# Attention probabilities of a scan-and-attention stage turned by 16-bit transposing transfers instead of TensorE

## The chip, the cores and the metric

One core of a Trainium2 chip runs the whole program. The metric is device microseconds (us) of one execution. The kernel before was timed in three runs: 1071.51, 1073.46 and 1073.56 us, median 1073.46 us. The profile is of one more execution, with a time of its own.

## The reference, cut to what matters

The program is one residual block of a streaming encoder on 512 tokens of width 1024: a feed-forward half step, two token mixers side by side, an output projection, a second feed-forward half step, a norm. The change lies in the mixers, which share one input projection `p = h @ w_in`.

```python
# mixer A: RWKV-7, 8 heads x 64, state carried forward in time
state = state * w_t + (state a_t) b_t + v_t k_t ;  y_t = state r_t
# mixer B: forgetting attention, 8 heads x 64, blocks of 128 queries
s = einsum('bhqd,bhkd->bhqk', q_i, k) * scale
s = s + c_i[..., :, None] - cum[..., None, :]       # cumulative log-forget bias
pr = softmax(where(mask, s, -inf))
out = einsum('bhqk,bhkd->bhqd', pr, v)
x = x + (sigmoid(g_A) * (y_A @ P_A) + sigmoid(g_B) * (y_B @ P_B)) @ W_out
```

All is float32. A product wanted at that accuracy is made as three products of high and low halves (`whi`, `wlo` of a weight; `xh`, `xl` of the activations).

## The kernel before, in words

The change touches one stage, in which three things run together on one core:

- the scan of mixer A, 16 chunks of 32 tokens in a chain: `product_x`, `copy_x`, `product_u`, `copy_u`, `products_sy`, `scale_s`. TensorE and, in turn, VectorE or ScalarE hand each other one small tile (`spot`, `Xs`, `RD`).
- the attention of mixer B: four pairs of heads `p`, each with blocks of queries taken together as `(0, 1)`, `(2,)` and `(3,)`; inside a block the two heads are `q` = 0 and 1. That makes 12 blocks of two heads. A block has `w` = 384, 384 or 512 columns of keys. For one head the steps are `logits` (TensorE, into a PSUM tile `l`), `maximum` (VectorE, `mx`), `exp` (ScalarE, into `pts`), `divide` (VectorE, in place on `pts`), a transposition so that keys lie on the partitions, and `values` (TensorE, with `tr` and the values `vt`). `pts` has one buffer per head `q`, so the `exp` of a head's next block waits until the probabilities of the block before have left it. I call the way from one `exp` to the next `exp` of the same head a round; each head place `q` has 12.
- fills: 13 columns of `w_in` (`pq` for queries and keys, `pgt` for gates), 24 matmuls of 128x512 each. A column's weights come by an SP transfer into `raw`, ScalarE casts the high half (`whi`), VectorE subtracts (`wlo`).

Before the change the transposition is done on TensorE (`turn`: one transpose of 128x128 against `ident` for every 128 columns, into the PSUM tile that held the logits), and ScalarE copies the result to SBUF (`copy_t`). That is the ordinary form: 80 transposes and 24 copies.

Order: the stage is written as a list of operations (`plan.op`), and the table `ORDER` says in which order they are put into the program. TensorE, VectorE and ScalarE run exactly in that order; the costs handed to `op` are used only by whoever searched the table. The queues of GpSimd (POOL) and SyncE (SP) run in order too: SP carries the weight loads, the second half of `Tall` (`fetch`, eight small transfers after chunks 3 and 7), and prefetches for the next stage; POOL carries the stores of gates (`gsave<-gs`) and prefetches (`G<-gsave`, `ga<-gsave`) into tiles that the scan gives up. A waiting instruction holds back all that stand behind it in its queue. `PLACES` names the PSUM bank that each `spot` and `l` gets. Since most operations go through one helper, their line in the profile is L103; the names of the tiles tell them apart.

Transposing transfers are not new to the kernel. The feed-forward stages (L804) and the token-wise copy of the residual (`tokens`, L1099 to L1107) use them: a float32 tile is taken apart into two planes of 16-bit halves, one transfer on SP turns both, and the halves are joined again.

Of the kernel before, what the change touches and what calls it, by code (L numbers as in the profile page):

```python
# [9 lines left out]
F32 = mybir.dt.float32  # L10
F32R = mybir.dt.float32r
BF16 = mybir.dt.bfloat16
U16 = mybir.dt.uint16
# [6 lines left out]
P = 128  # L20
T = 512
D = 1024
KD = D // P
# [4 lines left out]
C = 32  # L28
# [20 lines left out]


ORDER = [int(n) for n in """
# [23 lines left out]
""".split()]  # L75
PLACES = {
    "pr": "0211021000210120210202202102010110120102020202202121010201001002012202100020210",
    "pf": "0120120022102102001201210201",
}


# [1 line left out]
def kernel(  # L83
# [6 lines left out]
    nc = tc.nc  # L90
# [64 lines left out]
    loads = []  # L155

    def load_raw(aps, kt, n):
        raw = wp.tile([P, kt, n], F32, tag="raw", name="raw", bufs=3)
        for c0, src in aps:
            loads.append(nc.sync.dma_start(raw[:, :, c0:c0 + src.shape[1]],  # L160
                                           src.rearrange("(k p) c -> p k c", p=P)))
        return raw
# [37 lines left out]
    def f32(ap):  # L200
        return ap.bitcast(F32)
# [4 lines left out]
    def on(do, *a):  # L206
        return lambda: do(*a)
# [884 lines left out]
    def win(c0, n=P):  # L1092
        return [(0, W[:, c0:c0 + n])]
# [15 lines left out]
    with ExitStack() as mx:  # L1109
# [447 lines left out]
                pool.tensor_copy(Ds[i][half(q), :, q, :],  # L1557
                                 ident[half(q), half(q)].unsqueeze(1).broadcast_to([64, NP, 64]))

        plan = Plan(pr=3, pf=2, pm=1, w=1, raw=3, t=4, gs=2, tr=2, Xs=2)  # L1560
        op = plan.op
        summed, gone = [op("SP", 0.0, None, later=us, frees=frees) for us, frees in ((3.0, ()), (3.5, ["w"]))]
        o = op("ACT", 0.69, b1.log, summed, rank=SCAN, takes=["t"], frees=["pf"])
# [131 lines left out]


        ready, weighed = {0: [summed], 1: [rooted]}, []

        class Held:
            pass  # L1700

        def weights(at):
            w = Held()

            def load():
                w.raw = load_raw(win(at), KD, P)

            def high():
                w.hi, w.lo = [wp.tile([P, KD, P], F32R, tag=tag, name=tag, bufs=2) for tag in ("whi", "wlo")]
                act.copy(w.hi[:], w.raw[:])  # L1710

            def low():
                dve.tensor_tensor(w.lo[:], w.raw[:], f32(w.hi[:]), op=ALU.subtract)

            o = op("SP", 0.05, load, rank=FILL, takes=["raw"], later=4.0 if len(weighed) > 2 else 0.0)
            o = op("ACT", 0.99, high, o, *weighed[-1:], rank=NEXT, takes=["w"])
            weighed.append(op("DVE", 1.18, low, o, rank=NEXT, frees=["raw"]))
            return w, weighed[-1]
# [71 lines left out]

        pts = t2.tile([P, 2, T], F32, tag="pt", name="pts")
        qb = [rp.tile([P, T], F32R, name="qb0", tag="la"), t2.tile([P, T], F32R, name="qb1", tag="qb1")]
        sees, turned, exps, copies, yb = [], ([], []), [], [], []

        class Pair:
# [38 lines left out]
        class Block:  # L1834

            def __init__(s, pair, bl):
                s.pair, s.bl = pair, bl
                s.at = {b: sum(c + 1 for c in bl[:j]) * P for j, b in enumerate(bl)}
                s.w = sum(b + 1 for b in bl) * P
                s.lp, s.tr = [None] * 2, [None] * 2  # L1840

            def logits(s, q):
                s.lp[q] = whole("pf", pf)
# [22 lines left out]
            def divide(s, q):  # L1866
                sums = s.pair.mx[q][:, NB + s.bl[0]:NB + s.bl[-1] + 1]
                dve.reciprocal(sums, sums)
                for b in s.bl:
                    n, _, sum_ = s.of(q, b)  # L1870
                    dve.tensor_scalar(pts[:, q, n], pts[:, q, n], sum_, None, op0=ALU.mult)

            def turn(s, q):
                for k in range(s.w // P):
                    pe.transpose(s.lp[q][:, k * P:(k + 1) * P], pts[:, q, k * P:(k + 1) * P], ident[:])

            def copy_t(s, q):
                s.tr[q] = t2.tile([P, T], F32, tag="tr", name="tr", bufs=2)
                act.copy(s.tr[q][:, 0:s.w], s.lp[q][:, 0:s.w])

            def values(s):
                for j, b in enumerate(s.bl):
                    for k in range(b + 1):
                        o = s.at[b] + k * P
                        for m in range(0, P, C):
                            h = s.pair.p * P + m
                            pe.matmul(s.lp[1][m:m + C, j * P:(j + 1) * P], vt[k][:, h:h + C],
                                      s.tr[m // 64][:, o:o + P], start=k == 0, stop=k == b, tile_position=(0, m))

            def copy_o(s):  # L1890
                dve.tensor_copy(s.pair.qp[:, s.bl[0] * P:(s.bl[-1] + 1) * P], s.lp[1][:, 0:len(s.bl) * P])

            def enter(s, operands):
                for q in range(2):
                    us = sum(0.455 * (b + 1) * P / T + 0.06 for b in s.bl)
                    sees.append(op("PE", us, on(s.logits, q), *operands[q], rank=SIDE, takes=["pf"]))
                lit = sees[-2:]
                for q in range(2):
                    o = []
                    for b in s.bl:  # L1900
                        n = (b + 1) * P
                        e = op("DVE", 0.15 + 1.07e-3 * n, on(s.maximum, q, b), lit[q], rank=SIDE)
                        o.append(op("ACT", 0.265 + 0.85e-3 * n, on(s.exp, q, b), e, *turned[q][-1:], rank=SIDE))
                    exps.extend(o)
                    us = 0.19 + sum(0.14 + 0.525e-3 * (b + 1) * P for b in s.bl)
                    o = op("DVE", us, on(s.divide, q), *o, rank=SIDE)
                    lit[q] = op("PE", 0.11 * s.w / P, on(s.turn, q), o, rank=SIDE, kind="t")
                for q in range(2):
                    turned[q].append(lit[q])
                o = [op("ACT", 0.08 + 0.82e-3 * s.w, on(s.copy_t, q), lit[q], *copies[-1:], rank=SIDE, takes=["tr"],  # L1910
                        frees=["pf"] * (1 - q)) for q in range(2)]
                copies.append(o[1])
                us = 0.248 * sum(b + 1 for b in s.bl)
                o = op("PE", us, s.values, *o, rank=SIDE, frees=["tr"] * 2, kind="m")
                return op("DVE", 0.08 + 1.06e-3 * len(s.bl) * P, s.copy_o, o, rank=SIDE, frees=["pf"])

        outs = []
# [306 lines left out]
```

## Time and profile before

| | |
|---|---|
| median of three runs | 1073.46 us |
| the profiled execution's own time | 1072.17 us |
| its span | 1070.5 us (1.7 us lie around it) |
| granted TensorE clock | 0.998 of full |
| the stage with the change | about 510 to 647 us |
| TensorE transposes of `pts` | 80, from 522.5 to 637.3 us |
| copies `tr<-l` on ScalarE | 24, 12.3 us busy |

How to read the profile: a row of the timeline gives start, length, engine, line, operation, tiles, count, and in brackets how long the engine was idle before and what released it. "PEld" is the load of a matmul's stationary operand, which overlaps the matmuls. A row of the chain gives start, length and what the chain of work that ended last was in. A row of stretches gives the busy time of each engine, then the granted clock, the share of the transfer engines and GB/s. "SPq" and "POOLq" are the queues' own work, the issuing of transfers.

### The profile page before, as it was taken

What the parts mean: (1) busy time and instruction counts of PE and PEld (TensorE: products, weight loads), DVE (VectorE), ACT (ScalarE), POOL (GpSimd) and SP (SyncE); (2) the same over time, 40 slices, a digit from 0 to 9 for tenths busy, and PEclk for the clock granted to TensorE, in tenths of its full rate; (3) what the DMA queues carried; (4) which work ended last, traced back from release to release, by engine and by line L of the source; (5) the groups of instructions that cost most, each with busy time, mean ns of one, the idle gap of its engine ahead of it and who ended that gap; (6) DMA issues with size and microseconds to landing.
All of it is one profiled execution on the core that took longest, in us unless ns stands there. A gap on an engine that the chain in (4) does not pass through costs nothing.

```text
span 1070.5 us, 16775 instructions
## 1 busy us (share of the span) xinstructions
PE 1060.1 (99%) x6234; PEld 868.1 (81%) x6234; DVE 830.6 (78%) x1155; ACT 719.1 (67%) x1123; POOL 224.2 (21%) x275
## 2 busy tenths in 40 slices
PE   9999999999999999999999999999999999999997
PEld 7888888888887887888888787888888888888886
DVE  7997776789865698878777777866798766799874
ACT  6768767775655766445888876554578768676554
POOL 1221220134203202312000121136311212114210
PEclk9999999999999999999999999999999999999999
DMA  7999999989946443444312344666979999979972
GB/s 213 262 190 230 225 205 250 201 195 186 235 119 174 111 114 101 131 128 119 89 47 73 100 129 147 190 170 160 296 186 210 205 235 225 207 211 201 236 188 80
DMA packets 180112, 186.57 MB, mean 174 GB/s; under 512 B 50110, under 2 KB 116222, under 8 KB 180030
## 3 DMA queue, kind: packets, MB, share of 16 engines
q1 hardware_dynamic: 145902, 113.92, 37.0%
q0 software_dynamic: 33392, 70.14, 34.2%
q10 hardware_dynamic: 736, 1.45, 0.4%
q8 instruction: 49, 0.80, 0.3%
q14 instruction: 33, 0.27, 0.1%
HBM read 163.51 MB, written 12.52 MB: 164 GB/s over the span
## 4 chain that ended last, share of the span: by engine, by line
PE 86%; DVE 7%; ACT 3%; issue 2%; DMA 2%; SPq 0%; DVEq 0%; POOL 0%; ACTq 0%; POOLq 0%
PE P L103 32%; PE P L175 6%; PE P L177 6%; PE P L176 6%; PE pgt L103 5%; PE l L103 3%; PE spot L103 3%; PE pq L103 3%; PE ppj L103 2%; PE pk L175 2%; PE pk L177 2%; PE pk L176 2%; PE pw L176 1%; PE pw L175 1%; PE pw L177 1%
## 5 line engine op out<-in xcount | busy, mean ns | idle before, releaser
L103 PE MATMUL P<-sraw,q 128*128 128x512 f32 x344 | 91.3, 389 | 0.0
L103 PEld LDWEIGHTS P<-sraw,q 128*128 128x128 f32 x344 | 64.6, 188 | 13.4
L103 PE MATMUL P<-swhi,q 128*128 128x512 f32 x224 | 71.4, 390 | 0.1
L167 ACT CAST whi<-raw 128x1024 fp32r<-128x1024 f32 (+2 forms) x42 | 40.4, 961 | 45.2 <-issue 14.2
L103 PE MATMUL P<-sraw,wxh 128*128 128x512 f32 x200 | 67.7, 390 | 0.0
L103 PE MATMUL P<-swhi,wxh 128*128 128x512 f32 x144 | 56.6, 393 | 0.0
L168 DVE TENSOR_TENSOR wlo<-raw,whi 128x1024 fp32r<-128x1024 f32 (+2 forms) x43 | 48.5, 1127 | 10.4 <-ACT whi L167 9.1
L103 PE MATMUL P<-swhi,wxl 128*128 128x512 f32 x144 | 56.1, 390 | 0.0
L103 PE MATMUL P<-swlo,wxh 128*128 128x512 f32 x144 | 56.1, 389 | 0.0
L693 POOL DMA_DIRECT2D cb<-in_ffn_w_dram x20 | 24.1, 1207 | 145.8 <-DVE cd L103 78.4
L103 PE MATMUL P<-sraw,wxl 128*128 128x512 f32 x136 | 52.9, 389 | 0.0
L693 POOL DMA_DIRECT2D cd<-in_ffn_w_dram x24 | 29.3, 1221 | 112.6 <-DVE sraw L103 59.0
L103 PEld LDWEIGHTS P<-swhi,q 128*128 128x128 f32 x224 | 42.0, 188 | 9.2 <-DVE q L103 0.6
L103 DVE TENSOR_TENSOR u<-P,u 128x512 f32<-128x512 f32 x52 | 33.3, 682 | 13.7 <-ACT u L103 13.7
L103 PEld LDWEIGHTS P<-sraw,wxh 128*128 128x128 f32 x200 | 37.5, 188 | 7.7
L103 PE MATMUL P<-swlo,q 128*128 128x512 f32 x112 | 43.6, 389 | 0.0
L103 ACT COPY RD<-spot 32x128 f32<-32x128 f32 (+2 forms) x128 | 39.9, 312 | 5.3 <-PE spot L103 2.3
L552 POOL DMA_DIRECT2D ca<-in_ffn_w_dram x16 | 19.3, 1205 | 95.0 <-DVE swlo L103 65.6
L177 PE MATMUL pk<-xh,wlo 128*128 128x512 f32 x96 | 37.5, 392 | 1.0 <-DVE wlo L168 1.0
L175 PE MATMUL pk<-xh,whi 128*128 128x512 f32 x96 | 38.1, 396 | 0.4 <-DVE u L1257 0.4
L176 PE MATMUL pk<-xl,whi 128*128 128x512 f32 x96 | 37.4, 390 | 0.0
L177 PE MATMUL P<-swhi,wxl 128*128 128x512 f32 x96 | 37.3, 389 | 0.0
(630 smaller groups left out, 3435.2 us busy)
## 6 DMA issues: line engine op xcount, KB each, us to landing
raw<-in_w_in_dram SPq DMA_DIRECT2D x40, 512.0 KB
cc<-in_ffn_w_dram SPq DMA_DIRECT2D x36, 512.0 KB
cb<-in_ffn_w_dram POOLq DMA_DIRECT2D x36, 512.0 KB, 6.6
cb<-in_ffn_w_dram SPq DMA_DIRECT2D x32, 512.0 KB
cd<-in_ffn_w_dram POOLq DMA_DIRECT2D x32, 512.0 KB, 7.8
ca<-in_ffn_w_dram POOLq DMA_DIRECT2D x32, 512.0 KB, 8.4
ca<-in_ffn_w_dram SPq DMA_DIRECT2D x20, 512.0 KB
cd<-in_ffn_w_dram SPq DMA_DIRECT2D x18, 512.0 KB
```

What stands on the lines that cost most here:

```text
L103: q.last = do(*a, **kw)
L167: (hi_eng or act).copy(hi[:], raw[:])
L168: (eng or dve).tensor_tensor(lo[:], raw[:], hi[:].bitcast(F32), op=ALU.subtract)
L175: pe.matmul(ps, whi, xhi, start=first, stop=False, skip_group_check=onto)
L176: pe.matmul(ps, whi, xlo, start=False, stop=False, skip_group_check=onto)
L177: return pe.matmul(ps, wlo, xhi, start=False, stop=last, skip_group_check=onto)
L552: nc.gpsimd.dma_start(s.sum[g], src, accum_op=ALU.add)
L693: nc.gpsimd.dma_start(to, s.block(b, n, h), accum_op=ALU.add)
```

## The change

The transposition leaves TensorE. For each of the 24 block-and-head units:

1. `apart`, POOL: the float32 words of `pts` are copied as 16-bit halves into two planes (768 or 1024 halves per partition).
2. `turn`, SP: one transposing transfer writes the planes, turned, over `pts`.
3. `joined`: the halves are put together into `tr`, by VectorE for `q` = 0 and by ScalarE for `q` = 1.

The next `exp` of that head now waits for `joined`. The planes take one of the three `raw` buffers, so the weight columns keep two. `values` writes a PSUM tile of its own, so the tile of the logits is free after `exp`. `ORDER` and `PLACES` are replaced as a whole.

```diff
 ORDER = [int(n) for n in """
-172 1 191 173 0 174 6 175 379 176 374 11 192 372 373 177 178 7 179 381 375 376 14 5 210 377 378 380 12 8 9
...
+0 172 191 14 1 173 372 174 11 374 6 175 376 373 176 378 375 377 177 381 379 7 380 12 386 178 383 382 384 15
...
-        plan = Plan(pr=3, pf=2, pm=1, w=1, raw=3, t=4, gs=2, tr=2, Xs=2)
+        plan = Plan(pr=3, pf=2, pm=1, w=1, raw=2, t=4, gs=2, tr=2, Xs=2)
...
+        raws = [wp.tile([P, KD, P], F32, tag="raw", name="raw", bufs=3) for _ in range(3)]
+        planes = raws.pop().rearrange("p k t -> p (k t)").bitcast(U16).rearrange("p (q c) -> p q c", q=2)
...
+        JOIN, valued = ("DVE", "ACT"), []
...
+            def apart(s, q):
+                s.parts[q] = planes[:, q, 0:2 * s.w]
+                pool.tensor_copy(s.parts[q].rearrange("p (s c) -> p s c", s=2),
+                                 pts[:, q, 0:s.w].bitcast(U16).rearrange("p (c s) -> p s c", s=2))
+
             def turn(s, q):
-                for k in range(s.w // P):
-                    pe.transpose(s.lp[q][:, k * P:(k + 1) * P], pts[:, q, k * P:(k + 1) * P], ident[:])
-
-            def copy_t(s, q):
+                s.turned[q] = pts[:, q, 0:s.w].bitcast(U16)
+                nc.sync.dma_start(s.turned[q].rearrange("p (a t) -> p a t", t=P), s.parts[q], transpose=True)
+
+            def joined(s, q, copy):
                 s.tr[q] = t2.tile([P, T], F32, tag="tr", name="tr", bufs=2)
-                act.copy(s.tr[q][:, 0:s.w], s.lp[q][:, 0:s.w])
+                copy(s.tr[q][:, 0:s.w].bitcast(U16).rearrange("p (c s) -> p s c", s=2),
+                     s.turned[q].rearrange("p (s c) -> p s c", s=2))
...
-                    lit[q] = op("PE", 0.11 * s.w / P, on(s.turn, q), o, rank=SIDE, kind="t")
+                    o = op("POOL", 0.1 + 3.4e-3 * s.w, on(s.apart, q), o, rank=SIDE)
+                    o = op("SP", 1.3, on(s.turn, q), o, rank=SIDE, later=4.0)
+                    eng = JOIN[q]
+                    copy = act.copy if eng == "ACT" else dve.tensor_copy
+                    lit[q] = op(eng, 0.1 + (2.1e-3 if eng == "DVE" else 1.85e-3) * s.w, on(s.joined, q, copy), o,
+                                *copies[-1:], rank=SIDE, takes=["tr"])
...
-                o = [op("ACT", 0.08 + 0.82e-3 * s.w, on(s.copy_t, q), lit[q], *copies[-1:], rank=SIDE, takes=["tr"],
-                        frees=["pf"] * (1 - q)) for q in range(2)]
+                o = lit
```

What moves in the queues, at three places. On TensorE, before, in the first pair's blocks `(2,)` and `(3,)` (a transpose of three tiles reads `ident,pts`; `pq` is a fill, `l<-tr,vt` the value products):

```order
2097 L103 MATMUL l_4294<-tr,vt_3836 32x128 x8
2098 L103 MATMUL l_4294<-tr,vt_3838 32x128 x4
2099 L103 MATMUL l_4291<-ident,pts 128x128 x3
2100 L103 MATMUL pq<-xh_2573,whi 128x512
2101 L103 MATMUL pq<-xl_2574,whi 128x512
2102 L103 MATMUL pq<-xh_2573,wlo 128x512
```

All 24 such rows are gone; the value products of the first block now stand alone between scan and fills, and nothing on TensorE belongs to the transposition.

On POOL, in the second half of the stage, after (`raw<-pts` is `apart`; the rest are stores of gates and prefetches, the only things that stood there before):

```order
137 L1882 COPY raw<-pts 128x768 x2
138 L1788 DMA gsave<-gs 128x512
139 L1988 DMA G_2527<-gsave 128x512
140 L1882 COPY raw<-pts 128x768
141 L1788 DMA gsave<-gs 128x512
142 L1882 COPY raw<-pts 128x768
143 L1788 DMA gsave<-gs 128x512
144 L1882 COPY raw<-pts 128x1024 x2
145 L1788 DMA gsave<-gs 128x512
146 L1988 DMA G_2528<-gsave 128x512
147 L1882 COPY raw<-pts 128x768 x2
```

The copies of the third and fourth pair stand behind stores and prefetches that wait for a gate's `gs` or for a `G` tile of the scan.

On SP, around chunk 3 of the scan, after (`pts<-raw` is the transposing transfer, `raw<-in_w_in_dram` a weight load, `Tall<-Td` the eight transfers of `fetch`):

```order
127 L1887 DMA_TRANSPOSE pts<-raw 128x6x128
128 L1887 DMA_TRANSPOSE pts<-raw 128x8x128
129 L1417 DMA Tall<-Td 32x4x32 x2
130 L1710 DMA raw<-in_w_in_dram 128x8x128
131 L1417 DMA Tall<-Td 32x4x32
132 L1887 DMA_TRANSPOSE pts<-raw 128x8x128
133 L1417 DMA Tall<-Td 32x4x32 x5
134 L1887 DMA_TRANSPOSE pts<-raw 128x6x128 x2
135 L1710 DMA raw<-in_w_in_dram 128x8x128
```

Before, the same stretch of SP held loads and `Tall<-Td x8` only; now transfers of the attention stand between them and behind them.

More of the change, by code (lines that the diff above doesn't have):

```diff
@@ L51 @@
 ORDER = [int(n) for n in """
[23 rows of a table removed]
[23 rows of a table added]
 """.split()]
 PLACES = {
-    "pr": "0211021000210120210202202102010110120102020202202121010201001002012202100020210",
-    "pf": "0120120022102102001201210201",
+    "pr": "0211010102002012101211212011211210210200200021012121201020101101102121121020212",
+    "pf": "0102120121010210212012020120110101221212",
 }
@@ L1705, in load @@
             def load():
-                w.raw = load_raw(win(at), KD, P)
+                w.raw = raws.pop(0)
+                for c0, src in win(at):
+                    loads.append(nc.sync.dma_start(w.raw[:, :, c0:c0 + src.shape[1]],
+                                                   src.rearrange("(k p) c -> p k c", p=P)))
             def high():
@@ L1713, in low @@
                 dve.tensor_tensor(w.lo[:], w.raw[:], f32(w.hi[:]), op=ALU.subtract)
+                raws.append(w.raw)
             o = op("SP", 0.05, load, rank=FILL, takes=["raw"], later=4.0 if len(weighed) > 2 else 0.0)
@@ L1839, in __init__ @@
                 s.w = sum(b + 1 for b in bl) * P
-                s.lp, s.tr = [None] * 2, [None] * 2
+                s.lp, s.tr, s.parts, s.turned = [[None] * 2 for _ in range(4)]
             def logits(s, q):
@@ L1871, in divide @@
                     dve.tensor_scalar(pts[:, q, n], pts[:, q, n], sum_, None, op0=ALU.mult)
+            def apart(s, q):
+                s.parts[q] = planes[:, q, 0:2 * s.w]
+                pool.tensor_copy(s.parts[q].rearrange("p (s c) -> p s c", s=2),
+                                 pts[:, q, 0:s.w].bitcast(U16).rearrange("p (c s) -> p s c", s=2))
             def turn(s, q):
-                for k in range(s.w // P):
-                    pe.transpose(s.lp[q][:, k * P:(k + 1) * P], pts[:, q, k * P:(k + 1) * P], ident[:])
-            def copy_t(s, q):
+                s.turned[q] = pts[:, q, 0:s.w].bitcast(U16)
+                nc.sync.dma_start(s.turned[q].rearrange("p (a t) -> p a t", t=P), s.parts[q], transpose=True)
+            def joined(s, q, copy):
                 s.tr[q] = t2.tile([P, T], F32, tag="tr", name="tr", bufs=2)
-                act.copy(s.tr[q][:, 0:s.w], s.lp[q][:, 0:s.w])
+                copy(s.tr[q][:, 0:s.w].bitcast(U16).rearrange("p (c s) -> p s c", s=2),
+                     s.turned[q].rearrange("p (s c) -> p s c", s=2))
             def values(s):
+                s.out = whole("pf", pf)
                 for j, b in enumerate(s.bl):
@@ L1886, in values @@
                             h = s.pair.p * P + m
-                            pe.matmul(s.lp[1][m:m + C, j * P:(j + 1) * P], vt[k][:, h:h + C],
+                            pe.matmul(s.out[m:m + C, j * P:(j + 1) * P], vt[k][:, h:h + C],
                                       s.tr[m // 64][:, o:o + P], start=k == 0, stop=k == b, tile_position=(0, m))
             def copy_o(s):
-                dve.tensor_copy(s.pair.qp[:, s.bl[0] * P:(s.bl[-1] + 1) * P], s.lp[1][:, 0:len(s.bl) * P])
+                dve.tensor_copy(s.pair.qp[:, s.bl[0] * P:(s.bl[-1] + 1) * P], s.out[:, 0:len(s.bl) * P])
             def enter(s, operands):
@@ L1895, in enter @@
                     us = sum(0.455 * (b + 1) * P / T + 0.06 for b in s.bl)
-                    sees.append(op("PE", us, on(s.logits, q), *operands[q], rank=SIDE, takes=["pf"]))
+                    sees.append(op("PE", us, on(s.logits, q), *operands[q], *valued[-2:-1], rank=SIDE, takes=["pf"]))
                 lit = sees[-2:]
@@ L1902, in enter @@
                         e = op("DVE", 0.15 + 1.07e-3 * n, on(s.maximum, q, b), lit[q], rank=SIDE)
-                        o.append(op("ACT", 0.265 + 0.85e-3 * n, on(s.exp, q, b), e, *turned[q][-1:], rank=SIDE))
+                        o.append(op("ACT", 0.265 + 0.85e-3 * n, on(s.exp, q, b), e, *turned[q][-1:], *o[-1:], rank=SIDE,
+                                    frees=["pf"] * (b == s.bl[-1])))
                     exps.extend(o)
@@ L1906, in enter @@
                     o = op("DVE", us, on(s.divide, q), *o, rank=SIDE)
-                    lit[q] = op("PE", 0.11 * s.w / P, on(s.turn, q), o, rank=SIDE, kind="t")
+                    o = op("POOL", 0.1 + 3.4e-3 * s.w, on(s.apart, q), o, rank=SIDE)
[4 more added lines that the diff above has]
+                                *copies[-1:], rank=SIDE, takes=["tr"])
                 for q in range(2):
                     turned[q].append(lit[q])
-                o = [op("ACT", 0.08 + 0.82e-3 * s.w, on(s.copy_t, q), lit[q], *copies[-1:], rank=SIDE, takes=["tr"],
-                        frees=["pf"] * (1 - q)) for q in range(2)]
+                o = lit
                 copies.append(o[1])
                 us = 0.248 * sum(b + 1 for b in s.bl)
-                o = op("PE", us, s.values, *o, rank=SIDE, frees=["tr"] * 2, kind="m")
+                o = op("PE", us, s.values, *o, rank=SIDE, takes=["pf"], frees=["tr"] * 2, kind="m")
+                valued.append(o)
                 return op("DVE", 0.08 + 1.06e-3 * len(s.bl) * P, s.copy_o, o, rank=SIDE, frees=["pf"])
```

44 rows, old and new, of the table ORDER are left out of this document.

## The prediction

> **What bounds the kernel now.** I read the engine totals first, then the stretch of the stage, then the chain there, then the timeline of one block.
>
> ```profile
> span 1070.5 us, 16775 instructions
> PE 1060.1 (99%) x6234; PEld 868.1 (81%) x6234; DVE 830.6 (78%) x1155; ACT 719.1 (67%) x1123; POOL 224.2 (21%) x275
> ```
>
> ```profile
> 510.00:647.00 137.00, 137.00 (x1896) 110.29 (x1895) 101.06 (x255) 113.87 (x296) 12.70 (x23) 1.00 0.32 94
> ```
>
> TensorE is busy in 99% of the span and in all 137.0 us of the stage, at full clock. There VectorE has 101.1 us of work (36 us idle), ScalarE 113.9 (23 idle), POOL 12.7. So the stage lasts as long as TensorE's queue, and work taken from that queue shortens it, as long as nothing else becomes longer than what is left. That condition is the question here.
>
> **TensorE's credit.** From the chain inside the stage (its steps run from end to end of the work):
>
> ```profile
> 522.60 0.48 PE l L103 x3
> 523.08 0.70 PE pq L103 x3
> 537.39 0.79 PE l L103 x24
> 562.93 1.13 PE l L103 x27
> 572.36 0.59 PE l L103 x4
> ```
>
> The first row is a burst of three transposes between scan and fill, 0.48 us; the last a burst of four, 0.59. The fourth holds 24 value products and three transposes, 1.13 us against 0.79 for 24 products alone (third row), so right behind value products a burst costs 0.34. One transpose more costs 0.11 us (0.59 - 0.48). Lower bound: 80 x 0.11 = 8.8 us. Upper bound: 16 x 0.48 + 8 x 0.59 = 12.4 us. How much of the cost of switching goes too depends on the new neighbours; the two bursts seen between scan and the next work bear the full cost, one of three does not, so I take 11.0, nearer the upper end.
>
> **The round of one head.** What is removed from TensorE comes back as a longer round: `exp`, `divide`, `apart`, transfer, `joined`, and only then the next `exp` on the single `pts` buffer.
>
> ```profile
> L103 ACT ACTIVATE pts<-l,mx x32: 359/528/693, 514.9 to 633.6; 128x128 f32<-128x128 f32 x8, 128x256 f32<-128x256 f32 x8, 128x384 f32<-128x384 f32 x8, 128x512 f32<-128x512 f32 x8
> L103 DVE TENSOR_SCALAR pts<-pts,mx x32: 285/384/488, 521.2 to 634.7; 128x128 f32<-128x128 f32 x8, 128x256 f32<-128x256 f32 x8, 128x384 f32<-128x384 f32 x8, 128x512 f32<-128x512 f32 x8
> ```
>
> ```profile
> 557.50 0.37 ACT L103 ACTIVATE pts<-l,mx 128x128 f32<-128x128 f32 x1
> 558.22 0.20 ACT L103 ACTIVATION_READ_ACCUMULATOR pts<-l,mx 128x1 f32 x1
> 558.45 0.17 DVE L103 RECIPROCAL mx<-mx 128x2 f32<-128x2 f32 x1 [0.17 <-ACT pts L103]
> 558.66 0.55 DVE L103 TENSOR_SCALAR pts<-pts,mx 128x128 f32<-128x128 f32 x2
> ```
>
> The `exp` of a block `(0, 1)` takes 0.92 us (557.50 to 558.42), hand-over and `divide` 0.79 (to 559.21). For `(2,)` and `(3,)`, by the same rows and the longest lengths (0.69 and 0.49 at 512 columns), about 1.25 and 1.5 together.
>
> Transfer and splitting are shown by `tokens`, behind the stage, which turns 1024 halves per partition in the same way:
>
> ```profile
> 711.23 1.12 ACT L1102 COPY G<-xS 128x512 uint16<-128x512 uint16 x2
> 712.76 1.77 SPq L1103 DMA_TRANSPOSE G<-G  x1
> 717.56 1.89 POOL L1105 COPY G<-G 128x512 uint16<-128x512 uint16 x2 [1.57 <-DMA G<-G]
> 723.65 1.84 SPq L1103 DMA_TRANSPOSE G<-G  x1
> 728.14 2.19 POOL L1105 COPY G<-G 128x512 uint16<-128x512 uint16 x2 [1.30 <-DMA G<-G]
> 729.10 1.80 SPq L1103 DMA_TRANSPOSE G<-G  x1
> 735.15 1.43 POOL L1105 COPY G<-G 128x512 uint16<-128x512 uint16 x2 [3.61 <-DMA G<-G]
> 740.56 2.94 POOL L1105 COPY G<-G 128x512 uint16<-128x512 uint16 x2
> ```
>
> Hand-over to SP: 0.4 us (712.35 to 712.76). From the issue to the reader's start: 4.8, 4.5 and once 6.05 us; I take 4.6 for 1024 halves and, an estimate by size, 4.3 for 768. POOL's copy of 1024 halves: 1.43 to 2.94 us; I take 2.15, the middle of those shown, and 1.6 for 768.
>
> `joined` by VectorE is not in the trace. Bounds: one element a step as in the subtraction (1.22 us for 1024 elements, row below), or twice that speed, as `divide` runs (0.49 for 512). I take the slow end, since its halves are not contiguous: 1.22 and 0.92. ScalarE copies such halves at 1.0 us per 1024:
>
> ```profile
> 75.91 1.99 ACT L103 COPY p<-u 128x1024 uint16<-128x1024 uint16 x2
> ```
>
> Bare rounds: `(0, 1)` 0.92 + 0.79 + 1.6 + 0.4 + 4.3 + 0.92 = 8.9; `(2,)` 1.25 + 1.6 + 0.4 + 4.3 + 0.92 = 8.5; `(3,)` 1.5 + 2.15 + 0.4 + 4.6 + 1.22 = 9.9. Mean 9.1 us.
>
> What a round may take if all 11.0 us are to be kept: the first and last `exp` lie 118.7 us apart now (514.9 to 633.6), 10.8 a round. The last block's way from `exp` to `values` grows by about 7.5 us (its 9.9 against `exp`, `divide`, a burst of 0.59 and a copy near 0.6); the new order puts the first logits and `exp` earlier, by two groups of fills (0.70 each) and some copies, which I put at 3. So (118.7 - 11.0 - 7.5 + 3) / 11 = 9.4 us. The bare round leaves 0.3 of that for waiting in five queues.
>
> **What waits cost.** ScalarE was 83% busy in the stage and VectorE 74%, with instructions of up to 1.05 and 1.22 us; an arrival meets a busy engine in some 8 of 10 cases and waits half of a typical 0.6 us, an estimate of 0.25 us, and a round arrives there three times. SP adds its own:
>
> ```profile
> 541.07 3.67 SPq L1417 DMA_DIRECT2D Tall<-Td  x8
> ```
>
> These eight transfers hold SP for 3.67 us, 0.46 each; the order puts three, then five of them ahead of transposing transfers, twice in the stage: 2 x 1.5 us, some 0.25 a round. I drop what overlaps of the two and take 0.75 us in all. Loss: 11 x (9.1 + 0.75 - 9.4) = 5.0 us. With no waits at all nothing is lost; with 1.5 us a round, 13.2. When a round is late, VectorE or ScalarE stand at `joined` in their written order, with the scan's `copy_x`, `scale_s` and `copy_u` behind them, and TensorE waits for those.
>
> **VectorE and ScalarE.** ScalarE loses 24 copies (12.3 us) and gains 8 x 0.78 + 4 x 1.0 = 10.2: nothing. VectorE gains 8 x 0.92 + 4 x 1.22 = 12.2 us. POOL's copies slow it besides:
>
> ```profile
> 706.74 0.74 DVE L263 SCALAR_TENSOR_TENSOR xl<-xS,par,xh 128x512 fp32r<-128x512 f32 x1
> 712.19 1.19 DVE L263 SCALAR_TENSOR_TENSOR xl<-xS,par,xh 128x512 fp32r<-128x512 f32 x1
> 442.75 0.68 DVE L1257 TENSOR_TENSOR u<-pk,rstd 128x512 f32<-128x512 f32 x1
> 732.81 1.22 DVE L168 TENSOR_TENSOR wlo<-raw,whi 128x1024 fp32r<-128x1024 f32 x1
> 738.81 2.96 DVE L103 TENSOR_TENSOR wlo<-raw,whi 128x1024 fp32r<-128x1024 f32 x1
> ```
>
> The same operation takes 0.74 us alone and 1.19 beside a POOL copy; the subtraction 1.22 alone and 2.96 beside POOL. An operation that reads PSUM (`u<-pk`) keeps its 0.68. POOL copies for 24 x 1.8 = 43 us; if half of what VectorE does then is of the slowed kind, at 0.62 of its speed, it loses 43 x 0.5 x 0.38 = 8 us. Sum: 101 + 12 + 8 = 121 of 131 us. It fits, with a quarter of the idle time it had; I count no more for it than the waits above. The Trainium skill, "GPSIMD Engine Reference", section 8, has GpSimd contending with VectorE where VectorE's instruction reads two SBUF inputs or runs in a two-port mode. By that rule `divide` and the SBUF copies are slowed too; with three quarters in place of half the loss is 12 us, VectorE has 125, and the third rival gains. The rows show the two-input part.
>
> **At nothing.** Two `raw` buffers for three: a load holds its buffer from issue to subtraction.
>
> ```profile
> cb<-in_ffn_w_dram POOLq DMA_DIRECT2D x36, 512.0 KB, 6.6
> ```
>
> With 6.6 us for a load of that size, 1.05 for the cast and 1.22, that is 8.9 us; 13 columns in 137 us leave two buffers 21. If a load slips behind a waiting transfer on SP, what is late next is a fill, and TensorE stands in it. The PSUM tile of `values`: banks are given up earlier, at `exp`; no cost seen.
>
> **Forecast.** 1072.2 (the profiled execution, 1.3 below the median of 1073.46) - 11.0 + 5.0 = 1066.2 us.
>
> **Rivals.**
>
> First, all is hidden: waits of 0.3 us a round or less, 1061 us. For it: TensorE has always a fill to run. Against: five queues a round and little slack. Chance 0.22.
>
> Second, the round becomes the bound and eats the whole credit. Its place is the transfer: POOL's queue and SP's.
>
> ```profile
> 604.08 0.54 POOL L1782 DMA_DIRECT2D gsave<-gs  x1 [4.96 <-ACT gs L103]
> 642.19 0.54 POOL L1968 DMA_DIRECT2D G<-gsave  x1 [6.07 <-PE spot L103]
> ```
>
> Such waits cost nothing now; with `apart` behind them they stand in the round. It decides from 11.0 / 11 = 1.0 us of delay a round above 9.4, that is a mean round of 10.4. With every transfer at 6.05 us in place of 4.4, rounds are 9.1 + 0.75 + 1.65 = 11.5: 23 us lost, 1084; with half of them so, 14 lost, 1075. Against it: two of the three clear transfers landed in 4.5 to 4.8 beside weight loads, with the transfer engines busier than in this stage. Chance of a slower kernel 0.22, mostly at 1075 to 1079.
>
> The Trainium skill, "VectorE: DVE Perf Modes", section "The three transpose paths", speaks against the change: TensorE for 128x128 where PSUM will do, the transfer's path at 1309 ns a 16-bit block. By that figure six or eight blocks in turn would be 7.9 or 10.5 us, an estimate, and the kernel some 50 us slower. The rows above (eight blocks in 4.5 to 4.8 us) disagree; I give it 0.02 of those 0.22.
>
> Third, VectorE becomes the bound: if waits keep it idle for 10% as well, the stage lasts 121 / 0.9 = 134 us, 3 less than now: 1069. With 125 us of work it is 139: no gain. Speaks for it: the 2.96 us row. It fills the space between forecast and no change; chance of a time within 0.2% (2.1 us, about what a measurement here can tell from none) 0.16.
>
> **Chances.** Forecast, 1063 to 1070: 0.40. With the first rival, faster by over 0.2% is 0.62, same 0.16, slower 0.22. The range reaches below the first rival (12.4 us of credit, 1060) and to the second's milder form: 1060 to 1078, with 0.1 beyond it above and less below.
>
> **What would show it.** No `l<-ident,pts` on TensorE and about 11 us less of its work in the stage; `apart` at 1.6 and 2.15 us; `joined` on VectorE 0.9 and 1.2 us; from the transfer's issue to `joined` 4.3 to 4.8 us; rounds near 9.9 us; idle time of TensorE of some 5 us, ended by `RD`, `tr` or `Xs`. Rounds above 10.4 us or transfers of 6 us would make it wrong upwards; `apart` of 1.5 us for 1024 halves and VectorE's `joined` at half the length, downwards.

## The result, and the profile after

The changed kernel takes 1078.65 us (median of 7 runs, 1075.97 to 1081.09); the kernel before took 1072.12 in the same session. The ratio is 1.0057, 95% interval 1.0043 to 1.0071: slower by 0.6%, where 1066 was forecast. The profiled execution took 1077.94 us. Times below are medians; ratios are taken over all runs but two slow ones, one of e3 (1311.97 us, granted clock 0.752) and one of the kernel before in the session of e13 (1172.76 us, 0.85), and can differ a little from those of the medians.

First the engine totals and the stretch of the stage of the changed kernel (busy time of TensorE, its weight loads, VectorE, ScalarE, POOL, then granted clock, DMA share, GB/s):

```profile
span 1076.2 us, 16720 instructions
PE 1056.8 (98%) x6154; PEld 860.7 (80%) x6154; DVE 837.6 (78%) x1167; ACT 721.2 (67%) x1111; POOL 249.8 (23%) x299
```

```profile
510.00:647.00 137.00, 128.52 (x1748) 98.80 (x1746) 107.28 (x264) 112.28 (x275) 35.59 (x42) 1.00 0.53 119
```

TensorE was busy for all 137.0 us of this stretch; now 8.5 us of it are idle, at full clock, and the stage is longer all the same. VectorE has 107 us of work and ScalarE 112, so neither is full. Next the groups on the tiles of the round (durations as shortest/median/longest in ns, then first and last start), and the first matmul of the next stage:

```profile
L103 ACT ACTIVATE pts<-l,mx x32: 367/527/690, 513.6 to 638.2; 128x128 f32<-128x128 f32 x8, 128x256 f32<-128x256 f32 x8, 128x384 f32<-128x384 f32 x8, 128x512 f32<-128x512 f32 x8
...
L1882 POOL COPY raw<-pts x24: 822/828/1967, 516.5 to 640.6; 128x768 uint16<-128x768 uint16 x16, 128x1024 uint16<-128x1024 uint16 x8
L1887 SPq DMA_TRANSPOSE pts<-raw x24: 1211/1236/2062, 519.2 to 642.1; - x24
L103 DVE COPY tr<-pts x12: 602/610/760, 525.2 to 645.5; 128x768 uint16<-128x768 uint16 x8, 128x1024 uint16<-128x1024 uint16 x4
L103 ACT COPY tr<-pts x12: 1042/1082/1357, 527.8 to 647.8; 128x768 uint16<-128x768 uint16 x8, 128x1024 uint16<-128x1024 uint16 x4
```

```profile
L103 PE MATMUL yc<-V,center x6: 590/592/592, 652.5 to 654.6; 128*128 128x512 f32 x6
```

The `exp` instructions now span 124.6 us (513.6 to 638.2), 11.3 a round, where they spanned 118.7, 10.8 a round. The next stage's first `yc` came at 647.4 before. So of the 5.1 us by which it is later, the first `exp` gives back 1.3, the rounds take 5.9, and the way from the last `exp` to `yc` 0.5 (14.3 against 13.8).

Who waits shows in the list of waits of the stage (total us, times, longest):

```profile
ACT tr L103 <- DMA pts<-raw: 8.2, 5, 3.2
...
DVE tr L103 <- DMA pts<-raw: 4.5, 3, 2.5
```

VectorE and ScalarE stand 12.7 us at `joined` until a transfer has landed. What holds the transfer shows in the chain of work that ended last, here late in the stage (start, length, what):

```profile
609.54 1.24 DVE wlo L103
...
610.84 0.37 SPq L1710
...
611.65 5.63 DMA pts<-raw
...
617.31 1.36 ACT tr L103
...
621.52 1.24 DVE wlo L103
...
622.77 0.38 SPq L1710
...
623.25 5.19 DMA pts<-raw
...
628.46 1.04 ACT tr L103
```

A weight load (L1710) waits for the subtraction `wlo`, which frees one of the two `raw` buffers, and the transposing transfer waits behind the load, on the same queue. POOL's row for the first of these two:

```profile
607.16 1.04 POOL L1882 COPY raw<-pts 128x1024 uint16<-128x1024 uint16 x1 [2.15 <-DVE pts L103]
```

The halves were apart at 608.20 and the transfer was issued at 611.65, 3.45 us later. Over all 24 transfers this gap (end of `apart` to issue, from those rows one by one) adds up to 21.2 us; where SP stood free it is 0.03. Not all of it is due to loads: the pieces of `Tall` stand in the same queue.

### The profile page after: what moved, and what is told of

It reads as the page before. It is cut to its first block, busy times and chain, and to the rows that moved or that the text cites. A ratio compares the mean times of both kernels' runs of the same rounds, so it can differ in the third digit from the quotient of the medians.

```text
span 1076.2 us, 16720 instructions
## 1 busy us (share of the span) xinstructions
PE 1056.8 (98%) x6154; PEld 860.7 (80%) x6154; DVE 837.6 (78%) x1167; ACT 721.2 (67%) x1111; POOL 249.8 (23%) x299
## 5 line engine op out<-in xcount | busy, mean ns | idle before, releaser
L103 PEld LDWEIGHTS P<-sraw,q 128*128 128x128 f32 x344 | 64.6, 188 | 13.4
L168 DVE TENSOR_TENSOR wlo<-raw,whi 128x1024 fp32r<-128x1024 f32 (+2 forms) x43 | 48.5, 1127 | 10.4 <-ACT whi L167 9.1
L103 PE MATMUL P<-swhi,wxl 128*128 128x512 f32 x144 | 56.1, 390 | 0.0
L1882 POOL COPY raw<-pts 128x768 uint16<-128x768 uint16 (+1 forms) x24 | 25.2, 1050 | 92.0 <-DVE pts L103 63.3
```

The costliest lines, as they stand in the source:

```text
L103: q.last = do(*a, **kw)
L168: (eng or dve).tensor_tensor(lo[:], raw[:], hi[:].bitcast(F32), op=ALU.subtract)
L1882: pool.tensor_copy(s.parts[q].rearrange("p (s c) -> p s c", s=2), pts[:, q, 0:s.w].bitcast(U16).rearrange("p (c s) -> p s c", s=2))
```

## The experiments

Two theories stood at the start. Mine: the round of one head is the bound, by the transfer's place on SP's queue, with the weight loads. Rivals: the credit on TensorE was over-estimated; or the copies and joins, or the mere latency and traffic of the transfers, make the loss.

**e1: the credit alone.** In the kernel before:

```diff
-                for k in range(s.w // P):
-                    pe.transpose(s.lp[q][:, k * P:(k + 1) * P], pts[:, q, k * P:(k + 1) * P], ident[:])
+                pass
...
-                act.copy(s.tr[q][:, 0:s.w], s.lp[q][:, 0:s.w])
+                act.copy(s.tr[q][:, 0:s.w], pts[:, q, 0:s.w])
```

> The kernel before with the 80 TensorE transposes of the probabilities left out; ScalarE copies the untransposed probabilities to tr instead, so the transposition is what is missing. It measures the credit by itself. If TensorE is the bound and the transposes stand in its way for their whole 11.0 us: 1060 to 1063. If the credit was over-estimated (a rival cause of the miss): 1065 or more; at 1069 or more nearly the whole miss would lie here.

Measured 1066.25 us, 0.9945 (0.9931 to 0.9958), in the range named for an over-estimated credit. The credit is 6.1 us, not 11.0, and below the lower bound of 8.8. TensorE's timeline of the kernel before shows a smaller price than the chain did, read from start to start of neighbours:

```profile
522.53 0.55 PE L103 MATMUL l<-ident,pts 128*128 128x128 f32 x3
522.83 0.48 PE L103 MATMUL pq<-xh,whi 128*128 128x512 f32 x1
```

The next matmul starts 0.30 us after the burst, before the burst's own 0.55 us are over; the chain had 0.48 for this burst. Over all bursts this comes to 8.2 us. From 510 us to the first `yc` TensorE is busy for 129.9 us in e1 where it was busy for 137.4, 7.5 less, and 1.2 us of idle time appear in their place.

**e12: what the credit is made of.** As e1, but `for k in range(1)` keeps one transpose of each burst.

> As e1 (ScalarE copies the untransposed probabilities), but the first transpose of each of the 24 bursts stays on TensorE, its result unread. It splits the credit that e1 measured (6.1 us for 24 bursts with 80 transposes): if each transpose costs alike, 24 cost 1.8 us and this runs at 1067.5 to 1068.5; if the switch into and out of a burst costs, 1069.5 to 1072.

Measured 1067.45, 0.9956 (0.9944 to 0.9968), at the edge of the first range: 24 bursts of one transpose cost 1.2 us, 0.05 each; the other 56 cost 4.9, 0.09 each. The 1.2 us are not clear of the noise (the intervals of e1 and e12 overlap), so the split is rough; but going into and out of a burst costs nothing that can be seen, and the range for a cost of switching (1069.5 or more) was not met.

**e2: no transfer.** In the changed kernel:

```diff
-                s.turned[q] = pts[:, q, 0:s.w].bitcast(U16)
-                nc.sync.dma_start(s.turned[q].rearrange("p (a t) -> p a t", t=P), s.parts[q], transpose=True)
+                s.turned[q] = s.parts[q]
```

> The changed kernel without the 24 transposing transfers: the joins read GpSimd's planes directly, so the transposition is what is missing; the copies apart and the joins stay. My theory (the transfer and its place on SP's queue make the round of one head the bound): a round loses some 6.5 us of issue, wait and landing, the whole credit shows, 1060 to 1064. Rival (the copies on GpSimd, VectorE and ScalarE, or the new order, cost the time): 1072 or more.

Measured 1066.26, 0.9945 (0.9932 to 0.9957): above my range, far below the rival's, and the same floor as e1. Its `exp` group on `pts`:

```profile
L103 ACT ACTIVATE pts<-l,mx x32: 350/528/698, 513.0 to 626.4; 128x128 f32<-128x128 f32 x8, 128x256 f32<-128x256 f32 x8, 128x384 f32<-128x384 f32 x8, 128x512 f32<-128x512 f32 x8
```

So copies apart, joins and the new order cost nothing that can be seen beyond that floor, and all of the loss, 12.4 us (1078.65 - 1066.26), comes with the transfers. A round of 10.3 us (113.4 / 11) is what TensorE's remaining work leaves; 11.3 is 1.0 too long, 11 times.

**e3: SP for the transfers alone.**

```diff
-                for c0, src in win(at):
+                for c0, src in win(at) if len(loaded) < 3 else []:
...
-                o = op("SP", 0.4, on(fetch, nc.sync, c + 5, 4), e, later=4.0)
+                o = op("SP", 0.4, None, e, later=4.0)
```

> The changed kernel with its first two weight loads of this stage alone (later columns are computed from what is in the two buffers) and without the 16 Tall<-Td pieces on SP, so gates, later heads' q and k, and the second half of the scan are not the reference's; all instructions of the engines stay, in the same order. SP then carries nothing but the transposing transfers, and no 512 KB load is in flight beside them. My theory (transfers stand behind waiting loads on SP, some 21 us over 24 transfers, and land late behind them): rounds near 9.9 us in place of 11.3, 1062 to 1068. Rival (the bare transfer's latency and the joins make the round, the queue is harmless): within 2 us of the changed kernel, 1076 to 1080.

Measured 1068.93, 0.9963 (0.9950 to 0.9977), 0.9 us above my range, with `exp` from 512.4 to 627.5, 10.5 a round: 9.7 of the 12.4 us are back with all the transfers in place. It takes away waits and traffic at once; the next two tell these apart.

**e5 and e11: waits or traffic.** Loads of half of the rows, read twice by ScalarE and VectorE; e5 with four buffers, e11 with two:

```diff
+        raws = [r[:, a:a + KD // 2, :] for r in raws for a in (0, KD // 2)][:4]      # e11: for a in (0,)]
...
-                                                   src.rearrange("(k p) c -> p k c", p=P)))
+                                                   src[0:KD // 2 * P, :].rearrange("(k p) c -> p k c", p=P)))
...
-                act.copy(w.hi[:], w.raw[:])
+                act.copy(w.hi[:].rearrange("p (a k) t -> p a (k t)", a=2), twice(w.raw))
```

> The changed kernel with weight loads of this stage that bring half of a column's rows (256 KB; ScalarE and VectorE read that half twice, so lengths stay and the projections differ), so that the same memory holds four such buffers in place of two and no load has to wait for a subtraction. The order on the engines is the same. Theory A (two buffers on one queue with the transfers couple loads and transfers: each stands behind the other's wait): 1067 to 1071. Theory B (the transfer's own latency and the traffic of loads beside it make the round long): traffic is halved, waits are gone but not on the path, 1073 to 1077.

> As e5 (loads bring half of the rows, read twice), but with two buffers as in the changed kernel: the waits for the subtraction stay, the traffic is halved. If the waits for a buffer make the loss: 1076 to 1079. If the 512 KB in flight beside a transfer makes it: 1069 to 1072, as e5.

e5 measured 1069.79, 0.9989 (0.9975 to 1.0003), in the range of theory A; e11 1076.41, 1.0047 (1.0027 to 1.0066), in the range for waits. Half of the traffic alone (e11 against the changed kernel) is 2.2 us by the medians and not clear of the noise: the intervals overlap, and e11's twelve runs lie between 1072.70 and 1084.70. The buffers are worth another 6.6. e11's list of waits, taken on its slowest run (1084.70), still has ScalarE at the join:

```profile
ACT tr L103 <- DMA pts<-raw: 9.1, 4, 6.2
```

I had expected that four buffers free the loads of the wait; they do so only in part. Six of e5's loads in the stage still start within 0.1 us of the end of a subtraction, here with a transfer behind the load:

```profile
528.82 1.30 DVE L103 TENSOR_TENSOR wlo<-raw,whi 128x1024 fp32r<-128x1024 f32 x1
```

```profile
530.14 0.37 SPq L1715 DMA_DIRECT2D raw<-in_w_in_dram  x1
530.61 1.22 SPq L1893 DMA_TRANSPOSE pts<-raw  x1
```

The gaps ahead of the issues still add up to 16.2 us. What has gone are the loads that stand on SP late in the stage: e5's last is issued at 589.93, the changed kernel's last two at 610.84 and 622.77; the standing at joins falls from 12.7 to 3.0. So the number of buffers weighs more than the traffic. That it acts through the loads' place on SP, e5 does not show by itself; e6 below tests that with all buffers and bytes as they were.

**e4: loads behind the transfers.** Each load is issued right after the next transfer:

```diff
+                with tc.issue_after(t.ins):
+                    while behind:
+                        behind.pop(0).issue()
```

> The changed kernel with every weight load of this stage issued right behind the next transposing transfer instead of ahead of it; the order on the four engines is the same, and nothing is left out. My theory: of the 21 us that transfers wait on SP some 14 are due to loads that wait for the subtraction; without them the time falls to 1069 to 1074, unless late loads give TensorE a wait for whi. Rival (the wait on SP is not on the path): 1076 to 1081.

Measured 1082.50, 1.0096 (1.0082 to 1.0110): slower than the changed kernel, and above both of my ranges. Rows of the timelines of ScalarE, VectorE and TensorE, and TensorE in four stretches of 5 us (busy, granted clock, DMA share, GB/s):

```profile
524.26 1.04 ACT L103 CAST whi<-raw 128x1024 fp32r<-128x1024 f32 x1 [5.25 <-DMA raw<-in_w_in_dram]
```

```profile
525.33 1.23 DVE L103 TENSOR_TENSOR wlo<-raw,whi 128x1024 fp32r<-128x1024 f32 x1 [3.91 <-ACT whi L103]
...
526.95 0.60 DVE L103 COPY tr<-pts 128x768 uint16<-128x768 uint16 x1
```

```profile
525.64 1.11 PE L103 MATMUL spot<-ident,BK 128*128 128x128 f32 x4 [4.58 <-ACT BK L103]
```

```profile
515.00:520.00 5.00, 4.96 (x70) 1.00 0.35 87
520.00:525.00 5.00, 1.06 (x20) 0.89 1.20 202
525.00:530.00 5.00, 4.36 (x15) 0.50 0.22 56
530.00:535.00 5.00, 5.00 (x68) 0.93 0.20 39
```

The load is late now: ScalarE stands 5.25 us at the cast until it has landed, with the scan's copy `BK` behind it, and VectorE 3.9 us at `wlo`, with the join behind it. TensorE waits 4.58 us for `BK` and then runs at half clock. Either order on one queue makes the one wait for the other.

**e6 and e7: loads on another queue.** `nc.sync.dma_start` of the load becomes `nc.scalar.dma_start` (e6) or `nc.gpsimd.dma_start` (e7).

> The changed kernel with the 13 weight loads of this stage issued by ScalarE instead of SP; nothing left out, the other instructions keep their order. Theory A: transfers no longer wait behind loads nor loads behind transfers; ScalarE pays 13 issues and stands where a buffer isn't free yet. Net 1070 to 1076. Theory B (traffic and latency): no gain, 1078 to 1082.

> The same with the 13 loads issued by GpSimd, whose queue also holds the copies apart. Theory A: loads are freed of the transfers, but a load that waits for its buffer now holds up the next copy apart instead of the next transfer: part of the gain, 1071 to 1077. Theory B: 1078 to 1082.

e6 measured 1072.85, 1.0013 (1.0001 to 1.0025); e7 1076.78, 1.0042 (1.0024 to 1.0060), both in the range of theory A. e6 is 5.8 us faster than the changed kernel, with intervals that do not overlap; e7's gain is not clear of the noise. In e6 the gaps ahead of the 24 issues fall from 21.2 to 6.8 us, the standing at joins from 12.7 to 4.9. The Trainium skill, "DMA: Bandwidth & Descriptors", section "Issuing engines are not separate DMA queues", has it that issuing from several engines saves only the sequencer's time, which is usually small. Here it is 5.8 us: the time is a sequencer's standing, not its issuing. In e7 that standing moved to POOL, ahead of `apart`; from its list of waits:

```profile
POOL raw L1710 <- DVE wlo L103: 17.9, 5, 8.6
```

**e8: a faster join.** `JOIN = ("DVE", "DVE")`.

> The changed kernel with the second head's halves joined by VectorE too (0.61 to 0.76 us in place of ScalarE's 1.08 to 1.36); nothing left out. Both theories have the join in the round: 0.5 us less in each second head's round, 12 copies less on ScalarE (13.5 us), 12 more on VectorE (7.8 us): 1074 to 1078. Rival (VectorE is the bound): 1080 or more.

Measured 1087.91, 1.0144 (1.0122 to 1.0166), a miss: each second join is 0.5 us shorter and the kernel 9 us slower. Its waits:

```profile
ACT pts L103 <- DVE mx L103: 13.4, 7, 3.8
...
ACT pts L103 <- DVE tr L103: 7.1, 4, 3.0
```

```profile
DVE tr L103 <- DMA pts<-raw: 9.1, 5, 3.7
```

Both heads' joins now stand on VectorE, and behind a join that waits stands the other head's maximum, for which ScalarE waits (13.4 us). VectorE has 114 us of work in the 140 from 510 to 650, so it is not full. That its order is the cause is read from these rows; no run separates it.

**e9 and e10: the other waits.** To e6 (in e9) or to the changed kernel (in e10) are added:

```diff
-                        queue.dma_start(Tb[o:o + C, a_, at:at + n, o:o + C], tv[q, i, :, a_, c0:c0 + n])
+                        with tc.issue_after(turns[5 if c0 == 8 else 11].ins) if c0 else ExitStack():
+                            queue.dma_start(Tb[o:o + C, a_, at:at + n, o:o + C], tv[q, i, :, a_, c0:c0 + n])
...
-            nc.sync.dma_start(bons[p], bsave[p])
+            with tc.issue_after(last[0].ins):
+                nc.sync.dma_start(bons[p], bsave[p])
...
-            nc.gpsimd.dma_start(gslot[m], gsave[KD + m])
+            with tc.issue_after(last[1].ins):
+                nc.gpsimd.dma_start(gslot[m], gsave[KD + m])
```

> A candidate, nothing left out: the weight loads of this stage issued by ScalarE as in e6; the two groups of eight Tall<-Td pieces each held on SP until a fixed transposing transfer (the 6th, the 12th) has been issued; GpSimd's prefetches G<-gsave and SP's bons<-bsave held behind the last copy apart and the last transfer. In e6 rounds of 14.7 and 13.0 us stand where GpSimd waits for a place for a prefetch, and two transfers wait 2.1 us behind Tall pieces. If the time follows the rounds, some 4 us less than e6: 1068 to 1070. If the prefetches are then late for the next stage: 1072 or more.

> The same without the first edit: the loads stay on SP ahead of the transfers. By the rounds, some 3 to 4 us less than the changed kernel: 1073 to 1076; if the loads on SP hide the rest, 1077 to 1080.

e9 measured 1071.51, 0.9999 (0.9990 to 1.0007), between its two ranges; e10 1079.13, 1.0070 (1.0057 to 1.0083), in its second. e9's stage did end 3.2 us ahead of the kernel before (first `yc` at 644.2), and the next one lost it. Its ScalarE at a weight cast, and its TensorE in the last of two stretches:

```profile
652.81 0.62 ACT L103 CAST whi<-raw 128x512 fp32r<-128x512 f32 x1 [2.99 <-DMA raw<-in_fox_proj_dram]
```

```profile
640.00:650.00 10.00, 9.01 (x58) 1.00 1.04 370
650.00:660.00 10.00, 8.12 (x29) 0.83 0.40 117
```

The held prefetches moved in one cluster at 370 GB/s, with a 256 KB load behind them. e10 did the same: its first `yc` came at 648.4, 4.1 us before the changed kernel's, and ScalarE then waited 3.3 us for such a load. So e10 does not show that the two edits are worth nothing inside the stage.

**e13 and e14: the prefetches spread again.** e13 is e9 without the hold of `bons`, and `G<-gsave` is held behind the 16th `apart` (`aparts[15]`) only; e14 is e13 without that hold.

> As e9, but the prefetches are spread again: G<-gsave is held behind the 16th copy apart only (not the last), and bons<-bsave stands where it stood in the changed kernel. In e9 the first yc of the next stage came 3.2 us earlier than in the kernel before, and the next stage gave that back: ScalarE waited 3.0 us for a 256 KB load behind a cluster of prefetches, and the granted clock fell to 0.83 for 10 us. If the cluster did that: 1068 to 1070, faster than the kernel before. If the next stage is bound otherwise: 1071 to 1073, as e9.

> As e13 without the hold of G<-gsave: the loads on ScalarE and the Tall<-Td pieces behind the 6th and 12th transfers alone. GpSimd's wait ahead of the 15th and 16th copies apart stays (rounds of 13 to 14.7 us in e6). If the rounds are the bound there: 2 to 3 us more than e13, 1071 to 1072.5. If that wait is not on the path: as e13.

e13 measured 1068.05, 0.9962 (0.9948 to 0.9975), faster than both kernels; e14 1072.35, 1.0005 (0.9992 to 1.0018); both in the ranges for their first causes. The next stage of e13, its `exp`s, and ScalarE's wait at the join:

```profile
650.00:660.00 10.00, 9.84 (x43) 1.00 0.29 81
```

```profile
L103 ACT ACTIVATE pts<-l,mx x32: 367/528/690, 514.2 to 629.7; 128x128 f32<-128x128 f32 x8, 128x256 f32<-128x256 f32 x8, 128x384 f32<-128x384 f32 x8, 128x512 f32<-128x512 f32 x8
```

```profile
ACT tr L103 <- DMA pts<-raw: 1.2, 2, 0.9
```

10.5 us a round, gaps ahead of the issues of 3.0 us in all, standing at joins of 1.3. Of the 12.4 us, 10.6 are back with nothing left out: the same transfers run and the same bytes move, so what their traffic and latency cost as such lies within the 1.8 us that are left. e14 keeps POOL's wait at a prefetch, by the program for a tile that the scan gives up (the row itself names no releaser), with `apart` behind it (two rows of its POOL timeline):

```profile
588.89 0.54 POOL L1990 DMA_DIRECT2D G<-gsave  x1 [3.62 <-issue]
589.43 1.46 POOL L1884 COPY raw<-pts 128x768 uint16<-128x768 uint16 x1
```

That hold is worth 4.3 us between e13 and e14.

## Why the prediction was wrong, step by step

- **The credit (11.0, bounds 8.8 to 12.4): failed.** It is 6.1 (e1). Lengths of chain pieces, 0.11 us a transpose more and 0.48 a burst, were taken as what removal gives back. From start to start the bursts take 8.2 us in all, TensorE's busy time falls by 7.5, and 1.2 of that comes back as idle time. e12 shows 0.05 to 0.09 a transpose and no cost of switching.
- **What a round may take (9.4): failed, the other way.** I let the last block's way grow by 7.5 us and the start come 3 earlier; up to the next stage's first `yc` they moved by 0.5 and 1.3. (To the start of the last value product the way grew by 2.9, from 9.0 to 11.9.) With 6.1 of credit a round may take 10.3 (e2). Had this and the credit been all, my round of 9.1 + 0.75 would have cost nothing, and the forecast of 1066.2 would have come true from two errors that cancel.
- **The bare round (9.1): its parts off both ways, its sum about right.** `apart` took a mean of 1.05 us where I had 1.6 and 2.15; VectorE's `joined` 0.61 and 0.76 (0.92 and 1.22 forecast); ScalarE's 1.08 and 1.36 (0.78 and 1.0). The bounds for VectorE's were read from 1.22 us for 1024 elements and 0.49 for 512; these two alone differ by a factor of 1.2 an element, and only with the shortest `divide` of the row (0.29 us) does the slope come out at about half. The hand-over to a free SP took 0.03, not 0.4. From issue to the join's start it is 5.9 us on average, not 4.3 to 4.6; but it is 5.9 in e13 too, where engines hardly stand, so most of the difference there is VectorE and ScalarE being busy with other things.
- **Waits (0.75 a round) and "at nothing" (two `raw` buffers): the step that decided.** The sum put 5.0 us on the rounds; the loss is 12.4. SP's part of the waits was put at 0.25 us a round, for the pieces of `Tall` alone. With this stage's loads off SP (e6) the gap ahead of an issue is 0.28 us on average (6.8 / 24), so that part was sized about right; in the changed kernel it is 0.88 (21.2 / 24). The missing 0.6 comes with the loads. I had computed that two buffers are free for long enough (8.9 of 21 us) and did not ask when, in SP's order, the load stands waiting. I named a load that slips behind a transfer; the transfer behind a waiting load was the other half. e6 returns 5.8 us by removing that coupling alone, e3 and e13 9.7 and 10.6 by removing also what stands beside it.
- **The rivals.** The second came true, with its place (POOL's queue and SP's) and its milder time (1075 to 1079) met. Of its mechanism, POOL's wait for prefetches is shown (4.3 us between e13 and e14), slower transfers by traffic are not (2.2 in e11, within the noise); the load's wait for a buffer, with the transfer behind it, it lacked. The third fell: VectorE had 107 us of work in the stretch, not 121. Over the whole stage it is 109.6 (510 to 652.5), where 101.1 and the 7.9 of its joins make 109.0: of the 8 us for VectorE being slowed beside POOL less than 1 came. The row of 2.96 us from which that slowing was in part taken stood beside another operation of POOL (`acc<-acc,sq`) first, and beside the copy for its last 1.2 us only. The Trainium skill's figure for the transfer ("VectorE: DVE Perf Modes", "The three transpose paths") would, by the prediction's estimate, have made the kernel some 50 us slower; the last section sets it against a row.
- **The signs named** (rounds above 10.4, idle time of TensorE) came: 11.3 us, and 8.5 us idle where some 5 were expected. TensorE's work in the stage fell by 3.4 us (137.4 to 134.0), not by about 11.

Added up again with measured terms: 1072.2 - 6.1 + 12.4 = 1078.5, against 1077.94 in the profiled execution. This closes by construction, as both terms are differences from the same floor. The rounds are a check of their own: 124.6 - 113.4 = 11.2 us more from first to last `exp` than in e2, where the two profiled executions (1077.94 and 1067.00) differ by 10.9. The gains of the runs overlap and are not a sum. 1.8 us stay open between e13 and the floor.

## What to carry to other kernels

When a step moves to a DMA, draw up the issuing queue in its order and ask of each neighbour what it waits for: a load that waits for a buffer costs nothing until something urgent stands behind it. Price work taken off the bounding engine by leaving it out in a run, not by the length of its pieces in the chain. Give waiting transfers and waiting loads separate queues, the loads one in which nothing urgent stands behind them (POOL's, with the copies in it, was no help that can be seen), and spread the prefetches; here that turned +0.6% into -0.4%.

## What the runs showed of the hardware that was not expected

In e4 TensorE's last matmul before the stall ended at 521.06 and the next began at 525.64. The granted clock fell to 0.50 in between and was back at full at about 530.7 (stretches of TensorE, busy time, granted clock, DMA share, GB/s):

```profile
523.50:524.00 0.50, 0.00 (x0) 0.90 0.15 24
524.00:524.50 0.50, 0.00 (x0) 0.50 1.21 322
...
530.50:531.00 0.50, 0.50 (x3) 0.78 0.00 0
```

The Trainium skill, "TensorE: Matmul & The Clock Gate", section "Part 1: The HAM clock gate (the "warmup" mystery)", has half rate after an idle window of about 3.4 us; this trace agrees in kind, but here some 2.8 us of idle time (521.06 to about 523.9) were enough. A stall of 4.6 us so costs more than itself: some 5 us at half clock follow.

A transposing transfer of eight 16-bit blocks was read by ScalarE, which stood waiting, 3.8 us after its issue (changed kernel, SP's row and ScalarE's):

```profile
576.38 1.24 SPq L1887 DMA_TRANSPOSE pts<-raw  x1
```

```profile
580.19 1.36 ACT L103 COPY tr<-pts 128x1024 uint16<-128x1024 uint16 x1 [0.77 <-DMA pts<-raw]
```

That is at most 0.48 us a block, against the 1309 ns for a 128x128 block of "VectorE: DVE Perf Modes", "The three transpose paths", in the Trainium skill. VectorE interleaves 768 halves in 0.61 us and ScalarE in 1.08; GpSimd takes them apart in 0.83.
